# Two-layer hybrid trunk on one core: row sums of the layer norms and of the RMS norm moved by steps in the order of work

## The chip, the cores and the metric

The kernel runs on one core of a Trainium2 chip. The metric is the device time of one launch in microseconds (us), taken as the median of several runs. Before the change three runs gave 1219.54, 1220.56 and 1221.93 us. The engines are named as in the profile: PE is TensorE (PEld its weight loads), DVE is VectorE, ACT is ScalarE, POOL is GpSimd and SP issues the transfers.

## What is computed

The input x is 256 tokens by 1024 channels, in float32. Two layers follow each other, and a last RMS norm. Cut to what matters here, a layer is:

```
h = rms_norm(x, norm_w);  z = h @ w_in + b_in          # 20480 columns
y_ret  = (head_norm(retention(rq, rk, rv)) * ret_norm_w * silu(rg)) @ ret_w_o
y_att  = (merged_attention(aq, ak, av) * silu(ag)) @ att_w_o
c      = conv31(c_lin * sigmoid(c_gate)) + conv_dw_b
c      = silu(layer_norm(c, conv_norm_w, conv_norm_b))
y_conv = (c * silu(cg)) @ conv_w_o
gates  = sigmoid(mg)                                    # three times 1024 columns
x      = x + (gates0*y_ret + gates1*y_att + gates2*y_conv) @ w_out
```

Two norms matter for the change. `layer_norm` on the convolution's output c needs the mean of c over the 1024 channels of each token, then the mean of the squares of c less that mean. `rms_norm` at the start of layer 1 needs the mean of the squares of x, which exists only when layer 0 has ended.

## The kernel before

**Units.** All weights are cut into units of 256 columns by 1024 rows. `order()` writes the list of the units out by hand, per layer: cs0 cl0 cs1 cl1 cs2 cl2 (gate and linear half of the convolution's input), the units rq, rk, rv, rg, mr, yr of the retention, cs3 cl3, the units aq, ak, av, ma, ag of the attention, and at the end ya0 to ya3, mc0 to mc3, cg0 to cg3, yc0 to yc3 and wo0 to wo3. Here ya, yc and wo are the projections out of the attention, of the convolution and of the merged branches, mc is the merge gate of the convolution and cg its SiLU gate. The main loop goes through the list; unit n is the pair of a layer's kind and a number, and "step n" below is the loop's pass for unit n.

**A float32 product as three.** A weight tile is loaded (`raw`, issued by SP three steps ahead). `split(n + 2)` (L221, L222), two steps ahead, writes its rounded high part `whi` on ACT and the remainder `wlo` on DVE; there are five buffers of each half unit, so a cast waits until PE has left a buffer. The product then takes three matmuls for each tile: high by high, high by low and low by high. cs, cl, cg, rq and the like take 48 matmuls of 256 columns (L241, `gemm`); mr, ma, mc, yr, ya and yc go in couples of units and take 24 matmuls of 512 columns each (L275, `gemm_wide`), the first 12 for the first 128 tokens (t = 0) and the second 12 for the others (t = 1); wo goes in couples too (L298, `gemm_two`).

**What sets the order.** Each engine works its instructions off in the order in which the program writes them. Besides its own unit, a step carries out what was booked for it with `later(step, function, ..., at=queue)`. The queues are played at these places of a step: `after_split` right after the split of unit n + 2, `inside` in the middle of the unit's matmuls, `first` right behind its matmuls, `due` after the unit's results were taken out of PSUM, and `tail` at the end. In layer 1's step cs0 the split comes behind `first` (the flag `late`). `held` keeps the results of a unit in PSUM until `finish_held` takes them out. The convolution's 31 taps (L433) are put on DVE wherever a running credit allows it.

**Layer norm of c.** `ln_add` (L441 to L443) adds the channels on DVE, `ln_mean` lets PE sum over the partitions (`ss`, L326), scales the sum on DVE (`mean`, L448) and makes two diagonal matrices of it (`dg`, L347), and `ln_rows` lets PE spread them to all partitions (`rb`, L353). `ln_apply` (L457) then adds the row to c; `ln_square` squares on ACT (L361) and adds up on DVE (L363); `ln_rstd` does the sum, the power on POOL (L341) and the diagonals again, `ln_rows` the spreading, and `ln_apply` multiplies. In the last units cg0 to cg3, `gated` uses the result (L657).

**Change of layer.** `project` adds the product to x (`xt`, L701) after wo. Its inner function `rest` squares the new x (L361 on ACT, L363 on DVE) and splits x, times the norm's weight, into high and low part: `gx`, L373 on ACT and L374 on DVE. The first units of a layer work on this unscaled `gx`, so that they need not wait for the norm. `norm_diag` (`ss` on PE, `v` at L339, POOL, `dg`) and `norm_rows` (`rb` on PE, `rows` at L382 on ACT) make the norm's factor; `by_rstd` (`zr`, L403) applies it to the first units' results, and `scaled` (`hf` L392, `h` L395 and L313) writes the scaled input `h` for the units from rq0 on.

Of the kernel before, what the change touches and what calls it, by code (L numbers as in the profile page):

```python
# [13 lines left out]
ALU = mybir.AluOpType  # L14
# [28 lines left out]
C_ALL = C_MASK + 768  # L43

RATE = 3.0
H0 = ((2, (0, 2)), (4, (4, 6)))
H1 = ((1, (0, 2)), (3, (4, 6)))
UNSCALED = 3
WARM = 4

# [95 lines left out]
def trunk(ctx: ExitStack, tc, xp, wp, b_in, params, consts, out):  # L146
# [23 lines left out]
    pos = {u: n for n, u in enumerate(units)}  # L170
# [3 lines left out]
    first, inside, due, tail, after_split = (defaultdict(list) for _ in range(5))  # L174
    taps = []

    def later(n, fn, *a, at=due):
        at[n].append((fn, a))
# [137 lines left out]
    def pair_tile(name):  # L316
        return sb.tile([128, 2, S], F32, tag="tmp", name=name)
# [12 lines left out]
    def fold(v):  # L330
        DVE.tensor_tensor(v[:, 0], v[:, 0], v[:, 1], ALU.add)
        return v[:, 0]
# [23 lines left out]
    def add_squares(key, v, start, stop):  # L356

        if start:
            st[key] = sb.tile([128, 2, S], F32, tag="z", name="acc")
        sq = st[key] if start else pair_tile("sq")  # L360
        ACT.activation(sq, v, AF.Square)  # L361
        if not start:
            DVE.tensor_tensor(st[key], st[key], sq, ALU.add)  # L363
        if stop:
            st[key] = fold(st[key])

    def unscaled(l, k):

        if k == 0:
            st[l, "g"] = sb.tile([128, NK, 2, S], F32R, tag="gated", name="gx", bufs=1)  # L370
        g = st[l, "g"]
        w = col(l, P_NW + k) if l else xt[:, k:k + 1]
        ACT.mul(g[:, k, 0, :], x[:, k, :], w)  # L373
        DVE.scalar_tensor_tensor(g[:, k, 1, :], x[:, k, :], w, g[:, k, 0, :].bitcast(F32), ALU.mult, ALU.subtract)  # L374
# [323 lines left out]
    def project(l, i, n, p):  # L698
        k = 2 * i
        xs = x[:, k:k + 2]  # L700
        DVE.tensor_tensor(xs, p, xs, ALU.add)  # L701

        def rest():
            add_squares((l + 1, "sq"), xs, i == 0, i == 3)
            for q in range(2):
                unscaled(l + 1, k + q)
        if i < 2:
            later(n + 1, rest, at=after_split)
        else:
            rest()  # L710


    def turn_out(k):
# [83 lines left out]
    for l in range(DEPTH):  # L797
        for i in (0, 1, 2, 3):
            b = pos[l, "rq", i - i % 2]
            later(b + 3 + 2 * (i % 2), ret_scores, l, i)  # L800
            later(b + 6 + 2 * (i % 2), ret_out, l, i, at=first)
            later(b + 8 + 2 * (i % 2), ret_back, l, i, at=first)
        for pair in range(4):
            b = pos[l, "aq", pair]
            v = pos[l, "av", pair]
            for g in range(3):
                later(b + 2 * g + 3, att_scores, l, pair, g)
            later(v + 1, att_exp, l, pair)
            later(v + 2, att_share, l, pair)
            later(v + 4, att_turn, l, pair, 0, 0, at=first)  # L810
            later(v + 4, att_turn, l, pair, 0, 1, at=first)
            later(v + 5, att_pv, l, pair, 0, at=first)
            later(v + 5, att_turn, l, pair, 1, 0, at=first)
            later(v + 5, att_turn, l, pair, 1, 1, at=first)
            later(v + 6, att_pv, l, pair, 1, at=first)
        for part in range(2):
            later(pos[l, "yr", 3], by_residue, l, part, 0)
            later(pos[l, "cs", 3], by_residue, l, part, 4)
        y, c = pos[l, "ya", 0], pos[l, "mc", 0]
        later(y + 1, ln_add, l)  # L820
        later(y + 3, ln_mean, l, at=inside)
        later(y + 3, ln_rows, l)
        later(y + 3, ln_apply, l, ALU.add, (0, 2))
        later(y + 3, ln_square, l, (0, 2))
        later(c + 0, ln_apply, l, ALU.add, (4, 6))
        later(c + 0, ln_square, l, (4, 6))
        later(c + 1, ln_rstd, l)
        later(c + 2, ln_rows, l)
        later(c + 2, ln_apply, l, ALU.mult, (0, 2))
        later(c + 3, ln_apply, l, ALU.mult, (4, 6))  # L830
        b = pos[l, "cs", 0]
        if l:
            later(b, norm_diag, l, at=first)
            later(b + 1, norm_rows, l, at=first)
            later(b + 1, finish_held, at=first)
            for d, ks in H1:
                later(b + d, scaled, l, ks)
        else:
            later(b + 1, norm_diag, l, at=first)
            later(b + 2, norm_rows, l, at=inside)  # L840
            later(b + 2, finish_held, at=inside)
            for d, ks in H0:
                later(b + d, scaled, l, ks)

    def warm_up():

        z = sb.tile([128, S], F32, tag="bb", name="zero")
        DVE.memset(z, 0.0)
        p = ps.tile([128, S], F32, tag="S", name="warm", bufs=4)
        for _ in range(WARM):  # L850
            PE.matmul(p, z[:, 0:128], z, start=True, stop=True)
# [5 lines left out]
    with tc.manual_schedule():  # L857
        DVE.memset(mhalf, -0.5)
        warm_up()
        parts = ((0, 1), (1, 2), (2, 4), (4, 6), (6, 8))  # L860
        pieces = load(0, parts)
        for a, b in parts:
            lo, hi = (8 + a * S if a else 0), 8 + b * S
            SP.dma_start(xt[:, lo:hi], xp[:, lo:hi])
            next(pieces)
        all_of(pieces)
        all_of(load(1, ((0, 4), (4, 8))))
        SP.dma_start(cst[:, :C_COSR], consts[:, :C_COSR])
        SP.dma_start(prm[:, 0:P_CW], params[:, 0:P_CW])
        all_of(load(2))  # L870

        def prepare(a, b):
            for k in range(a, b):
                unscaled(0, k)
        split(0, parts, prepare)
        split(1)
        for k in (0, 2, 4, 6):
            add_squares((0, "sq"), x[:, k:k + 2], k == 0, k == 6)
        sg = sb.tile([128, 2], F32, tag="sm2", name="sg", bufs=4)
        ACT.activation(sg, mhalf, AF.Sigmoid)  # L880
        st["credit"] = 0.0
        for n, (l, kind, i) in enumerate(units):
            all_of(load(n + 3))
            if n == 0:
                SP.dma_start(prm[:, P_CW:], params[:, P_CW:])
                SP.dma_start(cst[:, C_COSR:C_DEC], consts[:, C_COSR:C_DEC])
            if n == 2:
                SP.dma_start(cst[:, C_DEC:], consts[:, C_DEC:])
            if kind == "av" and i < 4:
                bias_rows(l, units[n], AV + i * W)  # L890
            elif kind == "av" and i < 8:
                bias_rows(l, units[n], AV + i * W, AV + (i + 4) * W)
            elif kind in ("rv", "mr", "ma", "mc") and i % 2 == 0:
                bias_rows(l, units[n], COLS[kind][1] + i * W, COLS[kind][1] + (i + 1) * W)
            late = n < 3 or (kind, i) == ("cs", 0)
            if not late:
                split(n + 2)
            play(after_split, n)
            if kind in ("yr", "ya", "yc"):
                src = st[l, "gated"]  # L900
            elif kind == "wo":
                src = st[l, "mh"]
            elif kind == "aq" or kind in ("ak", "av") and i >= 4:
                src = st[l, "hp"]
            else:
                src = st[l, "g" if kind in ("cs", "cl") and i < UNSCALED else "h"]
            if n in couple:
                p = (gemm_two if kind == "wo" else gemm_wide)(n, src, lambda t, p: finish_half(n, t, p))
            elif kind == "av":
                p = gemm_values(n, src)  # L910
            else:
                p = gemm(n, src)
            play(first, n)
            if late:
                split(n + 2)
            if n < 2 or (kind, i) == ("cs", 0):
                held.append((n, p))
                continue
            if n not in couple:
                finish(n, p)  # L920
            elif couple[n][1]:
                finish_half(n, 1, p)
            play(due, n)
            st["credit"] = min(st["credit"] + RATE - COST[kind] - (0.6 if kind in ("cs", "cl") and i < UNSCALED else 0.0), 3.2)
            while taps and st["credit"] >= 0.79:
                fn, t = taps.pop(0)
                fn(t)
                st["credit"] -= 0.79
            play(tail, n)
        assert not (due or first or inside or taps), (list(due), len(taps))  # L930
# [44 lines left out]
```

## Time and profile before

| | |
|---|---|
| median of three runs | 1220.56 us |
| the profiled execution's own time | 1217.52 us |
| its span, first to last instruction | 1215.5 us |
| PE busy | 1197.6 us (99%), 8260 matmuls |
| DVE busy | 976.2 us (80%) |
| ACT busy | 751.1 us (62%) |
| transfers | 214.60 MB, 177 GB/s on the mean |
| mean granted clock of PE | 0.995 |

The profile is of one execution. A row of the timeline gives start, duration, engine, line, operation and `out<-in`, and in brackets the idle time ahead of it with what ended it. Consecutive alike instructions of an engine are merged into one row with a count. Matmuls are pipelined: one of 512 columns is listed with 0.39 us, though the next starts 0.23 us after it. So what a wait costs PE is read from start to start, less the usual distance. The granted clock has two levels here, 1.00 (2.4 GHz) and 0.50 (1.2 GHz).

### The profile page before, as it was taken

The numbers are of one execution on the slowest core, as the hardware profiler recorded it, in microseconds if no ns is written. First come the engines' busy times: TensorE is split into PE (matmuls) and PEld (weight loads), VectorE is DVE, ScalarE is ACT, GpSimd is POOL, SyncE is SP. The second block draws the span as 40 slices with busy tenths as digits, with TensorE's granted clock in tenths as the row PEclk, the third lists the DMA queues.
The fourth block names the chain that finished last, engine by engine and source line by source line (L and its number), as shares of the span: only waits on it lengthen the run. The fifth ranks groups of instructions, "written<-read, shape, count | busy, mean of one in ns | idle before, by whom it ended". The sixth has DMA issues, their size and how long they took to land.

```text
span 1215.5 us, 21472 instructions
## 1 busy us (share of the span) xinstructions
PE 1197.6 (99%) x8260; PEld 1116.8 (92%) x8260; DVE 976.2 (80%) x1702; ACT 751.1 (62%) x1116; POOL 9.2 (1%) x17
## 2 busy tenths in 40 slices
PE   9999999999999999999999999999999999999997
PEld 8999989999999989788999989899999999987987
DVE  6978799887888886766689787998887878767765
ACT  6635467878686756456455446586767686763652
POOL 0000000000000000000000000000000000000000
PEclk9999999999999999999999999999999999999999
DMA  8754576555555566555536564655555545565560
GB/s 301 239 191 134 162 210 195 164 182 162 165 177 167 160 191 182 182 180 179 187 123 190 165 196 138 213 191 169 174 162 175 163 168 168 185 182 182 184 189 35
DMA packets 129910, 214.60 MB, mean 177 GB/s; under 512 B 9872, under 2 KB 99728, under 8 KB 129680
## 3 DMA queue, kind: packets, MB, share of 16 engines
q1 hardware_dynamic: 129808, 213.24, 55.7%
q8 instruction: 64, 1.05, 0.3%
q14 instruction: 38, 0.31, 0.1%
HBM read 212.15 MB, written 1.05 MB: 175 GB/s over the span
## 4 chain that ended last, share of the span: by engine, by line
PE 90%; issue 7%; DVE 1%; ACT 1%; DMA 1%; SPq 0%; POOLq 0%; POOL 0%; DVEq 0%; ACTq 0%
PE g L241 47%; PE g L275 29%; PE g L256 4%; PE as L590 2%; PE g L298 2%; PE u L642 1%; PE pt L624 1%; PE rs L529 1%; PE u L637 1%; DVE wlo L222 0%; ACT whi L221 0%; DMA xt<-in_xp 0%; PE rs L531 0%; PE u L638 0%; PE rt L561 0%
## 5 line engine op out<-in xcount | busy, mean ns | idle before, releaser
L222 DVE TENSOR_TENSOR wlo<-raw,whi 128x1024 fp32r<-128x1024 f32 (+1 forms) x387 | 455.9, 1211 | 107.7 <-ACT whi L221 103.9
L221 ACT CAST whi<-raw 128x1024 fp32r<-128x1024 f32 (+1 forms) x387 | 391.8, 1042 | 197.9 <-PE g L275 109.1
L241 PE MATMUL g<-h,whi 128*128 128x256 f32 x1664 | 300.8, 283 | 0.0
L241 PEld LDWEIGHTS g<-h,whi 128*128 128x128 f32 x1664 | 257.3, 189 | 0.8
L241 PE MATMUL g<-h,wlo 128*128 128x256 f32 x832 | 235.1, 283 | 0.0
L241 PE MATMUL g<-hp,whi 128*128 128x256 f32 x1280 | 233.9, 285 | 0.0
L433 DVE SCALAR_TENSOR_TENSOR cacc<-cpad,prm,cacc 128x256 f32<-128x256 f32 x480 | 201.2, 477 | 0.5 <-ACT cacc L430 0.4
L241 PEld LDWEIGHTS g<-hp,whi 128*128 128x128 f32 x1280 | 200.3, 192 | 0.9
L241 PE MATMUL g<-hp,wlo 128*128 128x256 f32 x640 | 181.1, 283 | 0.0
L275 PE MATMUL g<-whi,h 128*128 128x512 f32 x512 | 166.3, 399 | 0.0
L241 PEld LDWEIGHTS g<-h,wlo 128*128 128x128 f32 x832 | 156.7, 188 | 0.0
L241 PEld LDWEIGHTS g<-hp,wlo 128*128 128x128 f32 x640 | 122.7, 192 | 0.0
L275 PE MATMUL g<-whi,gated 128*128 128x512 f32 x384 | 121.0, 391 | 0.0
L275 PEld LDWEIGHTS g<-whi,h 128*128 128x128 f32 x512 | 97.1, 190 | 21.9
L275 PE MATMUL g<-wlo,h 128*128 128x512 f32 x256 | 101.4, 396 | 0.0
L275 PEld LDWEIGHTS g<-whi,gated 128*128 128x128 f32 x384 | 72.1, 188 | 14.9
L275 PE MATMUL g<-whi,hp 128*128 128x512 f32 x256 | 82.3, 393 | 0.0
L241 PE MATMUL g<-gx,whi 128*128 128x256 f32 x384 | 73.0, 291 | 4.4 <-ACT gx L373 1.5
L500 DVE TENSOR_TENSOR zz<-zz,cst 128x512 f32<-128x512 f32 x48 | 33.2, 692 | 52.1 <-ACT zz L499 52.1
L275 PE MATMUL g<-wlo,gated 128*128 128x512 f32 x192 | 74.8, 389 | 0.0
L241 PEld LDWEIGHTS g<-gx,whi 128*128 128x128 f32 x384 | 61.6, 197 | 6.3 <-ACT gx L373 2.1
L497 ACT ACTIVATE z<-g,prm 128x256 f32<-128x256 f32 x96 | 45.6, 475 | 31.1 <-DVE cacc L433 12.0
(156 smaller groups left out, 1522.7 us busy)
## 6 DMA issues: line engine op xcount, KB each, us to landing
raw<-in_wp SPq DMA_DIRECT2D x222, 512.0 KB, 4.7
raw<-in_wp SPq DMA_DIRECT2D x323, 256.0 KB, 4.2
bb<-in_b_in SPq DMA_DIRECT2D x56, 128.0 KB, 4.3
cst<-in_consts SPq DMA_DIRECT2D x1, 1408.0 KB, 9.2
out_y<-o SPq DMA_DIRECT2D x4, 256.0 KB, 2.4
xt<-in_xp SPq DMA_DIRECT2D x3, 256.0 KB, 5.2
cst<-in_consts SPq DMA_DIRECT2D x1, 384.0 KB, 7.3
prm<-in_params SPq DMA_DIRECT2D x1, 360.0 KB, 6.9
```

What stands on the lines that cost most here:

```text
L221: ACT.copy(h, t)
L222: DVE.tensor_tensor(lo, t, h.bitcast(F32), ALU.subtract)
L241: PE.matmul(p[:, j], w, v, start=(k == 0 and i == 0 and j == 0), stop=(k == NK - 1 and i == 2 and j == 1))
L256: PE.matmul(p[:, j], a[:, k, u, r], v, start=(k == 0 and i == 0 and j == 0), stop=(k == NK - 1 and i == 2 and j == 1))
L275: PE.matmul(p, a[:, k, u, r], v, start=(k == 0 and i == 0), stop=(k == NK - 1 and i == 2))
L298: PE.matmul(parts[u][j], w, v, start=(k == 0 and i == 0 and (j == 0 or last)), stop=(k == NK - 1 and i == 2 and (j == 1 or last)))
L433: DVE.scalar_tensor_tensor(c[:, 2 * i + j], cp[:, j, t:t + S], col(l, P_TAP + (2 * i + j) * TAPS + t), c[:, 2 * i + j], ALU.mult, ALU.add)
L497: ACT.activation(z[:, j], p[:, j], AF.Identity, bias=b)
L500: DVE.tensor_tensor(zz, zz, two(cst[:, sin:sin + S]), ALU.mult)
L529: PE.matmul(s[:, 0:256], k[:, d, 0:128], q[:, d, :], start=(d == 0), stop=(d == 1))
L590: PE.matmul(s[:, r], q[:, j, t], k[:, j, t] if g else k[:, j, :], start=True, stop=True)
L624: PE.transpose(p[:, i, r * 128:r * 128 + 128], sm[:, r, o:o + 128], ident)
```

## The change

The layer norm's second and later parts are booked at other steps. With y the step of ya0 and c the step of mc0 (c = y + 4): the mean's row product goes from the end of step y + 3 into the middle of step c, the two additions of the row and the squares from y + 3 and c to the ends of the matmuls of c and c + 1, the variance from the end of step c + 1 to the middle of c + 3, its row product from the end of c + 2 to the middle of c + 4 (cg0), and the multiplications from c + 2 and c + 3 to step c + 4. This holds for both layers. At the change of layer, `rest` only splits x; the four squares of x are booked behind the matmuls of cs0 of the next layer. In layer 1 the norm's sum goes from behind cs0 into the middle of cl0, its row product from behind cl0 into the middle of cs1, cl0 is held like cs0, and the scaled `h` comes one step later (after steps cs1 and cs2). Layer 0's start stays as it was. No computation is added or left out.

```
-H0 = ((2, (0, 2)), (4, (4, 6)))
-H1 = ((1, (0, 2)), (3, (4, 6)))
+H = ((2, (0, 2)), (4, (4, 6)))
...
         def rest():
-            add_squares((l + 1, "sq"), xs, i == 0, i == 3)
             for q in range(2):
                 unscaled(l + 1, k + q)
         if i < 2:
             later(n + 1, rest, at=after_split)
         else:
             rest()
+        later(pos[l + 1, "cs", 0], add_squares, (l + 1, "sq"), xs, i == 0, i == 3, at=first)
...
         later(y + 3, ln_mean, l, at=inside)
-        later(y + 3, ln_rows, l)
-        later(y + 3, ln_apply, l, ALU.add, (0, 2))
-        later(y + 3, ln_square, l, (0, 2))
-        later(c + 0, ln_apply, l, ALU.add, (4, 6))
-        later(c + 0, ln_square, l, (4, 6))
-        later(c + 1, ln_rstd, l)
-        later(c + 2, ln_rows, l)
-        later(c + 2, ln_apply, l, ALU.mult, (0, 2))
-        later(c + 3, ln_apply, l, ALU.mult, (4, 6))
+        later(c + 0, ln_rows, l, at=inside)
+        later(c + 0, ln_apply, l, ALU.add, (0, 2), at=first)
+        later(c + 0, ln_square, l, (0, 2), at=first)
+        later(c + 1, ln_apply, l, ALU.add, (4, 6), at=first)
+        later(c + 1, ln_square, l, (4, 6), at=first)
+        later(c + 3, ln_rstd, l, at=inside)
+        later(c + 4, ln_rows, l, at=inside)
+        later(c + 4, ln_apply, l, ALU.mult, (0, 2), at=first)
+        later(c + 4, ln_apply, l, ALU.mult, (4, 6))
         b = pos[l, "cs", 0]
-        if l:
-            later(b, norm_diag, l, at=first)
-            later(b + 1, norm_rows, l, at=first)
-            later(b + 1, finish_held, at=first)
-            for d, ks in H1:
-                later(b + d, scaled, l, ks)
-        else:
-            later(b + 1, norm_diag, l, at=first)
-            later(b + 2, norm_rows, l, at=inside)
-            later(b + 2, finish_held, at=inside)
-            for d, ks in H0:
-                later(b + d, scaled, l, ks)
+        later(b + 1, norm_diag, l, at=inside if l else first)
+        later(b + 2, norm_rows, l, at=inside)
+        later(b + 2, finish_held, at=inside)
+        for d, ks in H:
+            later(b + d, scaled, l, ks)
...
-            if n < 2 or (kind, i) == ("cs", 0):
+            if kind in ("cs", "cl") and i == 0:
                 held.append((n, p))
                 continue
```

What this does to the order of the instructions is shown at three places. The changed file is one line shorter ahead of all of them, so each line number is one less there.

PE, layer 0, where ya3 ends and mc0 begins (`gated` is the input of ya, `h` that of mc), before:

```order
L275 MATMUL g<-wlo,gated 128x512
L275 MATMUL g<-whi,gated 128x512
L353 MATMUL rb<-dg,cst 128x128 x2
L275 MATMUL g<-whi,h 128x512
L275 MATMUL g<-wlo,h 128x512
```

PE, the same place after the change, in the middle of mc0:

```order
L274 MATMUL g<-whi,h 128x512 x2
L274 MATMUL g<-wlo,h 128x512
L274 MATMUL g<-whi,h 128x512
L352 MATMUL rb<-dg,cst 128x128 x2
L274 MATMUL g<-whi,h 128x512
```

The row product `rb` stood between ya3 and mc0; now the 12 matmuls of mc0's first half stand ahead of it.

DVE, layer 0, from the split of mc3 (before) to the last multiplication by the variance's row (`mg` is a merge gate, `gs` the SiLU gate of cg), before:

```order
L222 TENSOR_TENSOR wlo<-raw,whi 128x1024 x2
L669 TENSOR_TENSOR mg<-g,bb 128x512 x2
L339 TENSOR_SCALAR v<-ss 128x2
L347 TENSOR_SCALAR dg<-cst,r 128x128 x2
L222 TENSOR_TENSOR wlo<-raw,whi 128x1024 x2
L457 TENSOR_TENSOR cacc<-cacc,rb 128x512 x2
L222 TENSOR_TENSOR wlo<-raw,whi 128x1024 x2
L669 TENSOR_TENSOR mg<-g,bb 128x512 x2
L457 TENSOR_TENSOR cacc<-cacc,rb 128x512 x2
```

DVE, the same place after the change, from the splits of cg0 and cg1 on:

```order
L221 TENSOR_TENSOR wlo<-raw,whi 128x1024 x4
L668 TENSOR_TENSOR mg<-g,bb 128x512
L338 TENSOR_SCALAR v<-ss 128x2
L346 TENSOR_SCALAR dg<-cst,r 128x128 x2
L668 TENSOR_TENSOR mg<-g,bb 128x512
L221 TENSOR_TENSOR wlo<-raw,whi 128x1024 x2
L456 TENSOR_TENSOR cacc<-cacc,rb 128x512 x2
L656 TENSOR_TENSOR gs<-gs,cacc 128x512
L456 TENSOR_TENSOR cacc<-cacc,rb 128x512 x2
```

The variance's `v` and `dg` now stand behind the split of cg1, and the multiplications by its row stand among the work of cg0.

DVE at the change of layer, from the split of cl0 to the norm's sum, before:

```order
L222 TENSOR_TENSOR wlo<-raw,whi 128x1024 x2
L374 SCALAR_TENSOR_TENSOR gx<-xt,prm,gx 128x256 x2
L363 TENSOR_TENSOR acc<-acc,sq 128x512
L374 SCALAR_TENSOR_TENSOR gx<-xt,prm,gx 128x256 x2
L701 TENSOR_TENSOR xt<-g,xt 128x512
L363 TENSOR_TENSOR acc<-acc,sq 128x512
L374 SCALAR_TENSOR_TENSOR gx<-xt,prm,gx 128x256 x2
L701 TENSOR_TENSOR xt<-g,xt 128x512
L363 TENSOR_TENSOR acc<-acc,sq 128x512
L331 TENSOR_TENSOR acc<-acc 128x256
L374 SCALAR_TENSOR_TENSOR gx<-xt,prm,gx 128x256 x2
L339 TENSOR_SCALAR v<-ss 128x2
```

DVE, the same place after the change:

```order
L221 TENSOR_TENSOR wlo<-raw,whi 128x1024 x2
L373 SCALAR_TENSOR_TENSOR gx<-xt,prm,gx 128x256 x4
L700 TENSOR_TENSOR xt<-g,xt 128x512
L373 SCALAR_TENSOR_TENSOR gx<-xt,prm,gx 128x256 x2
L700 TENSOR_TENSOR xt<-g,xt 128x512
L373 SCALAR_TENSOR_TENSOR gx<-xt,prm,gx 128x256 x2
L362 TENSOR_TENSOR acc<-acc,sq 128x512 x3
L330 TENSOR_TENSOR acc<-acc 128x256
L221 TENSOR_TENSOR wlo<-raw,whi 128x1024 x4
L338 TENSOR_SCALAR v<-ss 128x2
L346 TENSOR_SCALAR dg<-cst,r 128x128 x2
```

The sums of squares moved behind the last `gx`, and four `wlo` (the splits of cs1 and cl1) moved ahead of `v`. ACT changes in the same way: eight `gx` in a row, then the four squares, then the casts.

## Rows read from the trace of the kernel before

**Rows 1.** What PE waited for: us in total, times, longest us.

```profile
PE rb L353 <- DVE dg L347: 5.7, 2, 2.8
PE g L241 <- ACT gx L373: 1.5, 3, 0.5
PE g L241 <- DVE gx L374: 1.5, 3, 0.8
```

**Rows 2.** Timeline of PE, layer 0, end of ya3 to mc0.

```profile
508.07 0.39 PE L275 MATMUL g<-whi,gated 128*128 128x512 f32 x1
...
511.29 1.19 PE L353 MATMUL rb<-dg,cst 128*128 128x128 f32 x4 [2.83 <-DVE dg L347]
...
514.95 0.39 PE L275 MATMUL g<-wlo,h 128*128 128x512 f32 x1
```

**Rows 3.** Timeline of DVE, layer 0, the same place.

```profile
510.67 0.15 DVE L448 TENSOR_SCALAR mean<-ss 128x2 f32<-128x2 f32 x1
510.85 0.48 DVE L347 TENSOR_SCALAR dg<-cst,mean 128x128 f32<-128x128 f32 x2
```

**Rows 4.** Timeline of PE, layer 1, the same place.

```profile
1112.81 0.68 PE L353 MATMUL rb<-dg,cst 128*128 128x128 f32 x4 [2.83 <-DVE dg L347]
...
1114.95 0.39 PE L275 MATMUL g<-wlo,h 128*128 128x512 f32 x1
...
1119.83 0.39 PE L275 MATMUL g<-wlo,h 128*128 128x512 f32 x1
```

**Rows 5.** Stretches behind both: length, busy of each engine, PEclk, DMA.

```profile
512.00:514.00 2.00, 2.00 (x8) 1.61 (x7) 1.86 (x3) 0.70 (x2) 0.00 (x0) 0.50 0.70 271
...
1112.00:1114.00 2.00, 1.20 (x7) 1.12 (x8) 1.93 (x6) 0.00 (x0) 0.00 (x0) 1.00 1.05 328
```

**Rows 6.** Timeline of PE, change of layer: end of wo3, cs0, cl0.

```profile
605.92 0.28 PE L298 MATMUL g<-mh,wlo 128*128 128x256 f32 x1
...
607.47 0.39 PE L241 MATMUL g<-gx,whi 128*128 128x256 f32 x1 [0.35 <-DVE gx L374]
...
614.95 0.39 PE L241 MATMUL g<-gx,whi 128*128 128x256 f32 x1 [0.80 <-DVE gx L374]
...
616.35 0.50 PE L326 MATMUL ss<-cst,acc 128*128 128x1 f32 x4
...
622.55 0.60 PE L353 MATMUL rb<-dg,cst 128*128 128x128 f32 x4
```

**Rows 7.** Timeline of ACT, change of layer.

```profile
604.70 1.05 ACT L221 CAST whi<-raw 128x1024 fp32r<-128x1024 f32 x1 [3.23 <-PE g L298]
...
606.19 0.89 ACT L373 ACTIVATE gx<-xt,prm 128x256 fp32r<-128x256 f32 x2
...
609.83 0.63 ACT L361 ACTIVATE sq<-xt 128x512 f32<-128x512 f32 x1 [1.42 <-DVE xt L701]
```

**Rows 8.** Timeline of DVE, change of layer and first units of layer 1.

```profile
606.93 0.88 DVE L374 SCALAR_TENSOR_TENSOR gx<-xt,prm,gx 128x256 fp32r<-128x256 f32 x2
607.72 0.69 DVE L363 TENSOR_TENSOR acc<-acc,sq 128x512 f32<-128x512 f32 x1
...
609.11 0.69 DVE L701 TENSOR_TENSOR xt<-g,xt 128x512 f32<-128x512 f32 x1
...
616.89 0.16 DVE L339 TENSOR_SCALAR v<-ss 128x2 f32<-128x2 f32 x1 [1.60 <-PE ss L326]
617.85 0.48 DVE L347 TENSOR_SCALAR dg<-cst,r 128x128 f32<-128x128 f32 x2 [0.80 <-POOL r L341]
618.25 4.62 DVE L222 TENSOR_TENSOR wlo<-raw,whi 128x1024 fp32r<-128x1024 f32 x4
...
639.43 1.67 DVE L392 SCALAR_TENSOR_TENSOR hf<-xt,prm,rows 128x256 f32<-128x256 f32 x4
641.01 1.46 DVE L313 TENSOR_TENSOR h<-hf,h 128x512 fp32r<-128x512 f32 x2
```

## The prediction

> **What bounds the kernel now.** I read the list of PE's waits first. PE is busy for 99% of the span, so time is won only where PE waits or runs at half clock. The list names two places: the mean's row product of the layer norm waited twice, 5.7 us together, for the diagonals from DVE; and the matmuls on `gx` waited six times, 3.0 us together, three times for ACT and three times for DVE [rows 1]. The first stands once in each layer, the second at the change of layer, the very places that the change edits. The starts of the matmuls show what these waits really cost, since the listed idle time leaves out the pipeline's refilling.
>
> *Layer norm.* The last matmul of ya3 starts at 508.07, the next instruction, `rb`, at 511.29 [rows 2]: 3.22 us, of which 0.23 is the usual distance, so 2.99 us are lost. Layer 1 has the same listed wait of 2.83 us [rows 4], so 2.99 again. DVE comes late because mean and diagonals stand in its queue behind a split and a merge: `mean` runs at 510.67, the diagonals end at 511.33 [rows 3].
>
> *Clock.* Behind this wait the clock is at 0.50 in layer 0 and at 1.00 in layer 1 [rows 5], though the wait was alike. From `rb` to the same later matmul PE took 514.95 - 511.29 = 3.66 us in layer 0 and 1114.95 - 1112.81 = 2.14 us in layer 1 [rows 2, 4]. The half clock cost 1.52 us.
>
> *Change of layer.* cs0 could have begun at 605.92 + 0.12 = 606.04 and ended at 616.35 [rows 6]: 10.31 us. From there, `ss` with its 0.36 us of distance and cl0 took until 622.55, so a unit takes (6.20 - 0.36)/48 = 0.12 us per matmul or 5.75 us unhindered. cs0 lost 10.31 - 5.75 = 4.56 us. The pattern behind it: `gx` of channels 0 to 3 is behind the split of cl0 on both engines; for the next channels, squares and their additions stand between the addition to x and `gx` [rows 7, 8].
>
> **The change part by part.**
>
> *1. The mean's row in the middle of mc0.* A 512-column matmul takes (1119.83 - 1114.95)/21 = 0.232 us [rows 4]. mc0 can start at 508.30, its first 12 matmuls end at 511.09. `rb` still starts when its diagonals allow it, at 511.29, since nothing ahead of them on DVE moved. Left of the wait: 0.20 us. The work of `rb` is the same before and after.
>
> *2. The variance's row in the middle of cg0.* It cost PE no wait before. Now `v` stands behind the split of cg1 and a merge gate. The second cast of cg1 needs a buffer that mc3 leaves at three quarters of its matmuls. From there: cast 1.05 [rows 7], `wlo` 4.62/4 = 1.16, merge gate 0.69 as for an addition of the same size, and from `v` to the end of `dg` 618.33 - 616.89 = 1.44 [rows 8], with hand-overs of about 0.1: 4.4 us. PE needs for its way to `rb` six matmuls of mc3 and half of cg0: 1.39 + 2.87 = 4.26 us. Left: a wait of 0.15 us. Below, it is 0 if the buffer is free earlier; above, about 1.2 if one more `wlo` comes in late. I take 0.17, nearest to the sum.
>
> *3. Applications and squares one or two steps later.* They lie on DVE and ACT beside PE's work. What needs them is yc0, four cg units of 5.75 us after the row product; the DVE work between is two multiplications and four products with `cg`, all below 1 us each. I cost it at nothing; its cover is these 20 us, and a delay would show as a wait of yc1 for `gated`. The two layer norms together give 2 x (2.99 - 0.20 - 0.17) = 5.2 us, and the half clock of layer 0 goes with its wait: 1.5 us.
>
> *4. Squares out of the way of gx.* The cast of cl0 ends at 605.75 [rows 7]; `gx` of channel 0 now begins there instead of at 606.19. That brings nothing: its low part starts on DVE at 606.93, behind a `wlo`, as before, and PE goes on at 607.47 as before [rows 6, 8]. By then 607.47 - 606.04 - 0.12 = 1.31 us are lost. From 607.47 on: four low parts end at 608.6; the third addition to x, which began at 609.11 behind an addition of squares, ends at 609.2; ACT, now without a square of 0.63 in front, has the next `gx` at 609.7 (0.47 each), DVE the low part at 610.2. PE gets to channel 4 at about 610.3: no wait, where two stood. The fourth addition ends at 611.2, `gx` at 611.7, its low part at 612.2; PE is at channel 6 at 611.75 and can go on with the low part at 612.28, by the same 0.53 from DVE's start to PE as in 606.93 to 607.47. It loses 0.4 us. The rest of cs0 takes 616.35 - 614.95 = 1.40 as before [rows 6], so cs0 ends at 613.68 instead of 616.35: **2.7 us**.
>
> *5. The norm's sum and row one half unit later in order.* ACT squares from 612.1 on (four at 0.62), DVE adds behind `gx`, three of 0.69 and a fold: done at about 615.8. PE reaches `ss` in the middle of cl0 at 613.68 + 2.87 = 616.55: no wait. Then four `wlo` (4.62 us) go ahead of `v`: to 620.4; with 1.44 the diagonals are there at 621.8. PE reaches `rb` in the middle of cs1 at 613.68 + 5.75 + 0.36 + 2.87 = 622.7: no wait, 0.9 us to spare.
>
> *6. Scaled h a step later, cl0 held.* No instruction is added. rq0 needs h of channels 4 to 7 at its middle: PE is there at about 646.0 (622.7 + 0.4 for `rb`, half of cs1, four units until rq0, which is entered at 643.1, and half of rq0). On DVE, from 622 on: the split of cs2, two `zr`, `cpad`, a `zr`, `hf` 1.67, `h` 1.46 [rows 8], three taps, two splits, and the rest of cl1 and cs2, gives `hf` at 641 to 643.7 and the last low part at 645.1; before it was at 642.5. The order is a step later, PE 2.7 us earlier; 1.5 us are left for channel 4. I cost it at nothing. SP's queue keeps its order; the raw tile of cs2's second half waits for the `wlo` of cs1, which now comes at about 616.9 instead of 619.4, so it is not later.
>
> Sum: 5.2 + 1.5 + 2.7 = 9.4 us. Against the profiled execution, 1217.52, this is 1208.1. The median of the runs shown is 3.04 us above that execution; nothing in the change's places explains that, so I carry it: **1211.1 us**.
>
> **A rule against a row.** Two waits of 2.83 us, one followed by half clock and one not [rows 4, 5]: what a wait costs in clock is not a property of the program alone. The Trainium skill, page "TensorE: Matmul & The Clock Gate", section "What's actually happening", says that the gate's counting runs free of the kernel's start, so that the point at which the clock changes varies. The trace agrees as far as two waits can.
>
> **The rivals.**
>
> *A. The clock did otherwise in the timed runs.* If none of them has a half-clock stretch, the gain is 7.9 us (1212.7); if both layers have one, 10.9 (1209.6). The rows show each case once, so for two waits one stretch is the likeliest; runs spread by 2.4 us.
>
> *B. The gain at the change of layer is given back.* DVE has little spare time from cs0 to rk1; if `hf` or a split comes more than 1.5 us later than in part 6, rq0 waits, and 2.7 us go at most: 1213.8. For it: `v` behind four `wlo`, `scaled` a step later. Against it: the sums above.
>
> *C. The rows' waits only move.* If `rb` in mc0 or in cg0 found its diagonals as late as today relative to PE, only the change of layer and perhaps the clock would be won: 1217.9 to 1216.3. Against it: DVE's queue ahead of the first diagonals is unchanged and PE has 2.8 us more work before them.
>
> *D. The change doesn't do what it says.* The squares need only x, so in ACT's queue they start right behind `gx`, not after cs0. Should they wait for cs0's end, `ss` comes 0.8 to 1.6 us late: 1212 to 1213.
>
> *E. Slower: DVE becomes the bound at layer 1's start.* A lack there is paid at rq0's middle, in one piece. To lose 9.4 us and 2.4 more, DVE must be 1.5 + 11.8 = 13.3 us later than in part 6, two and a half units' worth. Nothing in the rows comes near: the last low part of `h` moves by 2.6 us.
>
> **How the numbers follow.** A change below 0.2% (2.4 us) can't be told from none in a measurement of this kernel. Forecast with all parts 0.60; A 0.14; B 0.12; C 0.05; D 0.03; E 0.04; 0.02 for small waits that eat the sum. The range reaches from A with its larger gain, less 2 us for the bounds of parts 1, 2 and 4, to between B and C: 1207.5 to 1216.5. Faster: forecast, A, B, D and a part of C: 0.90; same: the rest of C and the last: 0.06; slower: E: 0.04.
>
> **What would show it.** The waits of `rb` for `dg` fall from 5.7 us to below 1, in mc0 and cg0; no half clock before the kernel's end; the waits for `gx` go from 3.0 us to below 2, with none left at channel 4; cs0 takes 7.6 us; squares start before cs0's end; no wait at rq0. Wrong would be: a new wait above 1 us at `rb` in cg0 or cs1, at rq0 or at yc1.

## The result and the profile after

The changed kernel takes 1207.99 us (median of four runs, 1207.48 to 1208.45) against 1220.14 us for the kernel before (1219.54 to 1221.93) beside it: a ratio of 0.9905, 95% interval 0.9890 to 0.9919, so 12.15 us or 1.0% less. The forecast was 1211.1 us, 9.4 us less. The profiled execution after took 1207.90 us with a span of 1206.0 us. Against the profiled execution before, the span fell by 9.5 us, where the prediction's sum has 9.4; the timed runs fell by 2.7 us more. The 1207.99 us lie in the predicted range, 0.5 us above its lower end.

The list of PE's waits after the change (us in total, times, longest us):

```profile
PE g L240 <- ACT whi L220: 1.9, 2, 1.6
PE warm L843 <- DVE zero L840: 1.2, 1, 1.2
PE g L240 <- DVE gx L373: 0.9, 1, 0.9
PE g L240 <- DVE wlo L221: 0.8, 2, 0.6
```

Against [rows 1], the waits of `rb` for `dg` are gone from the list. Of six listed waits for `gx` one is left. The other rows belong to the first units of the launch.

The timeline of PE in layer 0, at the two row products of the layer norm:

```profile
510.79 0.40 PE L274 MATMUL g<-whi,h 128*128 128x512 f32 x1
511.21 0.68 PE L352 MATMUL rb<-dg,cst 128*128 128x128 f32 x4
...
534.48 0.28 PE L240 MATMUL g<-h,wlo 128*128 128x256 f32 x1
534.91 0.68 PE L352 MATMUL rb<-dg,cst 128*128 128x128 f32 x4
```

Both stand without listed idle time. From start to start the first loses 0.42 - 0.23 = 0.19 us, the second 0.43 - 0.12 = 0.31 us (0.19 and 0.30 in layer 1). DVE's rows for the two pairs of diagonals:

```profile
510.78 0.48 DVE L346 TENSOR_SCALAR dg<-cst,mean 128x128 f32<-128x128 f32 x2
...
533.43 0.15 DVE L338 TENSOR_SCALAR v<-ss 128x2 f32<-128x2 f32 x1
534.47 0.48 DVE L346 TENSOR_SCALAR dg<-cst,r 128x128 f32<-128x128 f32 x2 [0.90 <-POOL r L340]
```

The mean's diagonals come 0.07 us earlier than in [rows 3]: nothing about them became faster, PE only has 12 matmuls to do in the meantime. PE could have gone on with the second row at 534.60; the pair of the variance's diagonals is made from 534.47 to 534.95, and `rb` starts at 534.91.

The change of layer, PE, to be held against [rows 6]:

```profile
601.71 0.28 PE L297 MATMUL g<-mh,wlo 128*128 128x256 f32 x1
602.00 0.38 PE L240 MATMUL g<-gx,whi 128*128 128x256 f32 x1
603.25 0.39 PE L240 MATMUL g<-gx,whi 128*128 128x256 f32 x1 [0.87 <-DVE gx L373]
...
612.46 0.50 PE L325 MATMUL ss<-cst,acc 128*128 128x1 f32 x4
...
618.66 0.60 PE L352 MATMUL rb<-dg,cst 128*128 128x128 f32 x4
```

`ss` now stands in the middle of cl0, so cs0 ended 24 matmuls, 2.87 us, earlier: at 609.59. It began at 601.83 and took 7.76 us, against 10.31 before. And the queues that feed it, ACT and then DVE, against [rows 7] and [rows 8]:

```profile
601.45 1.70 ACT L372 ACTIVATE gx<-xt,prm 128x256 fp32r<-128x256 f32 x4
605.02 0.92 ACT L372 ACTIVATE gx<-xt,prm 128x256 fp32r<-128x256 f32 x2 [1.88 <-DVE xt L700]
607.09 0.91 ACT L372 ACTIVATE gx<-xt,prm 128x256 fp32r<-128x256 f32 x2 [1.15 <-DVE xt L700]
607.90 0.62 ACT L360 ACTIVATE acc<-xt 128x512 f32<-128x512 f32 x1
```

```profile
602.72 1.67 DVE L373 SCALAR_TENSOR_TENSOR gx<-xt,prm,gx 128x256 fp32r<-128x256 f32 x4
604.30 0.69 DVE L700 TENSOR_TENSOR xt<-g,xt 128x512 f32<-128x512 f32 x1
605.56 0.89 DVE L373 SCALAR_TENSOR_TENSOR gx<-xt,prm,gx 128x256 fp32r<-128x256 f32 x2 [0.58 <-ACT gx L372]
...
616.28 0.15 DVE L338 TENSOR_SCALAR v<-ss 128x2 f32<-128x2 f32 x1
617.24 0.48 DVE L346 TENSOR_SCALAR dg<-cst,r 128x128 f32<-128x128 f32 x2 [0.81 <-POOL r L340]
...
638.68 1.46 DVE L312 TENSOR_TENSOR h<-hf,h 128x512 fp32r<-128x512 f32 x2
```

The squares start at 607.90, while cs0 still runs; nothing makes them wait for it. The norm's diagonals end at 617.72, 0.9 us ahead of the `rb` that needs them. The scaled input is complete at 640.14, ahead of rq0's middle at about 642.2.

### The profile page after: what moved, and what is told of

It reads as the page before. It is cut to its first block, busy times and chain, and to the rows that moved or that the text cites. A ratio compares the mean times of both kernels' runs of the same rounds, so it can differ in the third digit from the quotient of the medians.

```text
span 1206.0 us, 21474 instructions
## 1 busy us (share of the span) xinstructions
PE 1194.5 (99%) x8260; PEld 1113.6 (92%) x8260; DVE 975.7 (81%) x1702; ACT 750.9 (62%) x1116; POOL 9.2 (1%) x17
## 4 chain that ended last, share of the span: by engine, by line
PE 91%; issue 6%; DVE 1%; DMA 1%; ACT 1%; SPq 0%; POOLq 0%; POOL 0%; DVEq 0%
PE g L240 47%; PE g L274 31%; PE g L255 4%; PE as L589 2%; PE g L297 2%; PE u L641 1%; PE pt L623 1%; DMA raw<-in_wp 1%; PE rs L528 1%; PE u L636 1%; ACT whi L220 0%; PE rs L530 0%; PE u L637 0%; PE rt L560 0%; PE r L540 0%
```

## Experiments

Two questions were left: where the 2.7 us come from that the timed runs won beyond the profile, and which moves the gain hangs on. Each kernel ran beside the kernel before on one chip: e1, e2, e3 and e5 share a median before of 1219.35 us (28 runs), the other four one of 1219.14 us (17 runs).

**The kernel before against itself (e1).** No edit.

> The kernel before, unchanged, against itself. Open: its timed runs (median 1220.14 us) lie 2.6 us above its profiled execution (1217.52), while those of the changed kernel lie at its own (1207.99 against 1207.90). Theory 1 (half clock): the timed runs hold more half-clock stretches behind PE's waits than the one, of 1.52 us, in the profiled execution; then runs differ by steps of about 1.5 us and the longer a run, the lower its mean granted clock (each such stretch takes about 0.0014 off 0.995 or more). Theory 2 (something outside the waits, such as transfers at the start): runs are longer at an unchanged mean clock.

It took 1218.34 us, ratio 0.9994 (0.9983 to 1.0004). Sorted by mean granted clock, the 40 runs of it (12 and the 28 beside) have these spans:

```
mean granted clock   runs   span, us
0.997 to 0.998          4   1214.1 to 1215.1
0.994 to 0.996         25   1215.0 to 1217.9
0.992 to 0.993         11   1218.2 to 1219.1
```

Sorted like this, the lower the clock, the longer the runs, as theory 1 has it; the steps of 1.5 us that it also foresaw are blurred. One trace against another need not follow this order: the trace of before has 1215.5 us at 0.995, that of this run 1216.8 us at 0.996. The mean also counts half clock at the start of the launch, which the first has (first row) and the second has not:

```profile
10.00:12.00 2.00, 2.00 (x11) 2.00 (x11) 1.80 (x5) 1.68 (x4) 0.00 (x0) 0.50 1.02 402
10.00:12.00 2.00, 2.00 (x17) 2.00 (x18) 2.00 (x5) 1.89 (x5) 0.00 (x0) 1.00 1.05 422
```

Both come to the first `ss` of the launch at 20.58 us all the same. Over the ten traces this moment lies between 20.2 and 21.1 us; so up to 0.9 us of the spread lies there, outside the waits, as theory 2 has it.

The profiled run of this kernel shows one more thing: the same wait of 2.83 us in layer 1, at 1.00 behind it in [rows 5], now has this behind it (stretches as there, then PE's timeline):

```profile
1112.00:1114.00 2.00, 2.00 (x7) 1.71 (x7) 1.94 (x4) 0.59 (x1) 0.00 (x0) 0.50 0.96 297
1114.00:1116.00 2.00, 2.00 (x6) 1.52 (x6) 1.09 (x2) 1.57 (x3) 0.00 (x0) 0.50 0.11 45
1116.00:1118.00 2.00, 2.00 (x8) 1.54 (x7) 0.83 (x1) 0.00 (x0) 0.00 (x0) 0.63 0.08 18
```

```profile
1111.40 1.19 PE L353 MATMUL rb<-dg,cst 128*128 128x128 f32 x4 [2.83 <-DVE dg L347]
...
1121.21 0.39 PE L275 MATMUL g<-wlo,h 128*128 128x512 f32 x1
```

This is the same matmul as the one at 1119.83 in [rows 4]: 9.81 us from `rb` here, 7.02 there. The half clock cost 2.79 us, where it cost 1.52 in layer 0 of the trace of before. One wait of one length is followed by a stretch that costs nothing, 1.5 or 2.8 us.

**Filling the wait instead of moving the work (e5).**

```
+    def fill(l):
+        p = ps.tile([128, 512], F32, tag="S", name="fill", bufs=4)
+        g = st[l, "gated"]
+        for _ in range(12):
+            PE.matmul(p, g[:, 0, 0, 0:128], g[:, 0, :, :], start=True, stop=True)
...
+        later(y + 3, fill, l)
         later(y + 3, ln_rows, l)
```

> The kernel before with 12 matmuls of 512 columns, whose result nobody reads, put on PE ahead of the mean's row product in both layers, where PE waits 2.99 us. They take 12 x 0.232 = 2.8 us, so PE loses the same time but is not idle. Theory 1: no half clock behind them; timed 1220.1 - 1.5 - 2.6 = 1216.0, span 1214.0 or less. Theory 2: only the one stretch of the profiled execution can go: 1218.6. If the clock is none of it: 1220.1, or a little more for the added matmuls.

Measured: 1216.09 us, ratio 0.9978 (0.9968 to 0.9988), 3.26 us below the kernel before. The time is that of theory 1; but the kernel before beside it was faster than the 1220.1 us from which both theories start, and as a saving 3.26 us stands between the 4.1 of theory 1 and the 1.5 of theory 2, with an interval from 1.5 to 3.9. The spread and the clock in the trace speak for theory 1, and so do the traces set side by side further below. Its span is 1213.9 us. Its ten runs lie within 1.8 us, those of the kernel before beside them within 5.1. PE in layer 0, then a stretch behind the filler in each layer:

```profile
508.20 2.88 PE L456 MATMUL fill<-gated 128*128 128x512 f32 x12
511.19 0.68 PE L354 MATMUL rb<-dg,cst 128*128 128x128 f32 x4
```

```profile
512.00:514.00 2.00, 2.00 (x10) 1.64 (x9) 1.76 (x3) 0.80 (x2) 0.00 (x0) 1.00 0.73 243
1112.00:1114.00 2.00, 2.00 (x10) 1.65 (x9) 1.78 (x3) 0.79 (x2) 0.00 (x0) 1.00 0.87 302
```

`rb` starts 6.2 us behind the `ss` ahead of it, as before, and no useful work moved; 24 matmuls that compute nothing are worth 3.3 us because PE is not idle. So in the timed runs the half clock behind the two layer norms costs a median run some 3.3 us (1.5 to 3.9 by the interval), where the profiled execution held 1.5.

**The layer norm's steps alone (e2).** The change's block of ten `later` lines, with the rest of the kernel before.

> Only the layer norm's steps are moved, the change of layer is as before. By the prediction's sum in rows 5.2 us of waits and 1.5 us of half clock go: span 1208.8. In timed runs, by theory 1 with the extra half clock behind the two layer norms: 1220.1 - 6.7 - 2.6 = 1210.8; if the extra half clock lies at the change of layer, or by theory 2: 1213.4. Rival (the layer norm's gain is not the larger part): above 1216.

1211.09 us, ratio 0.9932 (0.9918 to 0.9947): 8.26 us less. The time is at the first of the two values expected; the saving lies between the 9.3 and the 6.7 us that they stand for, and its interval (6.5 to 10.0) holds both, so this run doesn't decide between the theories. That the layer norm's part is the larger one is shown. In its waits `rb` is gone and `gx` is as before:

```profile
PE g L241 <- ACT gx L373: 1.5, 3, 0.5
PE g L241 <- DVE gx L374: 1.5, 3, 0.8
```

**The change of layer alone (e3).** The rest of the change, with the layer norm as before.

> Only the change of layer is moved, the layer norm's steps are as before. By the sum 2.7 us in the rows of cs0, and the two waits of 2.83 us at the layer norms stay. Timed: 1217.4 if the extra half clock lies at the layer norms or outside; 1214.8 if it lies at the change of layer.

1215.78 us, ratio 0.9974 (0.9963 to 0.9984): 3.57 us less, between the two values. The interval (2.0 to 4.5 us) holds the 2.7 us of the first and not the 5.3 of the second. Its runs spread over 4.9 us, as those of the kernel before do, and both waits of `rb` are still listed, 5.7 us. PE's timeline has the last matmul of wo3 and the `ss` in the middle of cl0, and the clock falls behind both layer norms (stretches as above):

```profile
606.23 0.28 PE L297 MATMUL g<-mh,wlo 128*128 128x256 f32 x1
...
616.98 0.50 PE L325 MATMUL ss<-cst,acc 128*128 128x1 f32 x4
```

```profile
512.00:514.00 2.00, 2.00 (x7) 1.73 (x8) 1.97 (x4) 0.25 (x1) 0.00 (x0) 0.50 1.00 369
1112.00:1114.00 2.00, 2.00 (x6) 1.57 (x5) 1.30 (x3) 1.44 (x3) 0.00 (x0) 0.50 0.45 154
```

cs0 takes 616.98 - 2.87 - 606.35 = 7.76 us, as in the changed kernel. Around the change of layer the clock is 1.00 in this trace and in that of before, so the extra half clock is not there. The two halves together give 8.26 + 3.57 = 11.8 us, the whole change 12.15 and 10.9 in its two measurements.

**The changed kernel again (e8).** No edit.

> The changed kernel, unchanged, on the chip of the runs beside it. 1207.99 us as in its first runs, all within 1 us of each other, since no wait of PE is left at the layer norms behind which the clock could fall.

1208.21 us, ratio 0.9913 (0.9901 to 0.9926), within 0.9 us of each other. The gain is 10.9 us on this chip.

**The mean's row alone (e6).** The variance and the multiplications go back to the steps they had, and so do the second of the two additions and its squares.

```
         later(c + 0, ln_rows, l, at=inside)
         later(c + 0, ln_apply, l, ALU.add, (0, 2), at=first)
         later(c + 0, ln_square, l, (0, 2), at=first)
-        later(c + 1, ln_apply, l, ALU.add, (4, 6), at=first)
-        later(c + 1, ln_square, l, (4, 6), at=first)
-        later(c + 3, ln_rstd, l, at=inside)
-        later(c + 4, ln_rows, l, at=inside)
-        later(c + 4, ln_apply, l, ALU.mult, (0, 2), at=first)
-        later(c + 4, ln_apply, l, ALU.mult, (4, 6))
+        later(c + 0, ln_apply, l, ALU.add, (4, 6))
+        later(c + 0, ln_square, l, (4, 6))
+        later(c + 1, ln_rstd, l)
+        later(c + 2, ln_rows, l)
+        later(c + 2, ln_apply, l, ALU.mult, (0, 2))
+        later(c + 3, ln_apply, l, ALU.mult, (4, 6))
```

> The changed kernel with only the first row product of the layer norm moved (into the middle of mc0, with the two additions it feeds); the variance and the multiplications keep the steps that they had before. If the gain at the layer norm is that one wait and its clock, as the prediction has it, this is as fast as the changed kernel: 1208.0, within 0.5. If the later steps of the variance and the multiplications are needed too (the rival: DVE comes too late for the row product behind mc2, or for cg0), a wait of 0.5 to 3 us stands there in each layer: 1209 to 1214.

1211.91 us, ratio 0.9946 (0.9932 to 0.9959): 3.7 us slower than the changed kernel. The rival holds, but at another place than it named. The first row is of PE's waits, the others of PE's timeline in layer 0:

```profile
PE ss L325 <- DVE acc L330: 2.6, 2, 1.3
```

```profile
520.35 0.40 PE L274 MATMUL g<-whi,h 128*128 128x512 f32 x1
522.07 0.58 PE L325 MATMUL ss<-cst,acc 128*128 128x1 f32 x4 [1.32 <-DVE acc L330]
```

It is not the row product but the sum over the partitions behind mc1. The squares are summed up 10.3 us behind `rb` here and 10.5 us in layer 1 of the kernel before; but PE, which did half of mc0 ahead of `rb` instead of standing still, now gets to `ss` 8.9 us behind `rb` instead of 11.7. From start to start 1.72 - 0.23 = 1.5 us go in each layer, 3.0 us in all; the second row product, back behind mc2, gives 0.6 of them back. The spans of the two traces differ by 3.4 us, of which 0.6 stand ahead of the first `ss` of the launch (20.97 against 20.42 us). The six runs spread over 3.0 us; whether the clock fell behind the new wait in some of them is not shown, for in the trace it didn't.

**gx ahead of the squares, in the same step (e7).**

```
         def rest():
-            add_squares((l + 1, "sq"), xs, i == 0, i == 3)
             for q in range(2):
                 unscaled(l + 1, k + q)
+            add_squares((l + 1, "sq"), xs, i == 0, i == 3)
```

> The kernel before, with only the two parts of the function after project exchanged: gx ahead of the squares, but both still in the steps of wo. If the order within a step were enough, cs0 would take 7.75 us in the rows, as in the changed kernel. By the queue sums the additions of squares still stand between the additions to x on DVE: gx of channel 4 comes 0.45 and that of channel 6 about 1.05 us earlier than before, and PE then waits about 0.2 us for the norm's sum: cs0 takes 9.2 us, against 10.3 before. Timed 0.9 us below the kernel before, if the clock behind the layer norms leaves that to be seen.

1218.10 us, ratio 0.9991 (0.9982 to 1.0000), 1.0 us less, which the interval hardly tells from none. The rows tell it. PE, then DVE:

```profile
606.33 0.28 PE L298 MATMUL g<-mh,wlo 128*128 128x256 f32 x1
...
613.59 0.91 PE L241 MATMUL g<-gx,whi 128*128 128x256 f32 x2 [0.69 <-ACT gx L373]
...
615.70 0.61 PE L326 MATMUL ss<-cst,acc 128*128 128x1 f32 x4
```

```profile
611.70 0.69 DVE L363 TENSOR_TENSOR acc<-acc,sq 128x512 f32<-128x512 f32 x1
612.31 0.68 DVE L701 TENSOR_TENSOR xt<-g,xt 128x512 f32<-128x512 f32 x1
```

From 606.45 to `ss` 9.25 us pass, as expected. An addition of squares still stands in front of the last addition to x on DVE, and `gx` of channel 6 waits for that. The exchange is worth 1.1 of the 2.6 us; the rest needs the squares behind every `gx`.

**The split of cl0 behind gx too (e4).** On top of the changed kernel:

```
             late = n < 3 or (kind, i) == ("cs", 0)
-            if not late:
+            last = (kind, i) == ("wo", 3)
+            if not late and not last:
                 split(n + 2)
...
+            if last:
+                split(n + 2)
             play(due, n)
```

> A version that may beat both: the changed kernel, with the split of cl0 put behind the last gx of wo's last step instead of ahead of the first. The 1.4 us that cs0 still loses at its first channels, where gx stands behind that split on both engines, and the 0.4 us at channel 6 should go: cs0 takes 5.8 us in the rows, 1206.2 timed. Rival: the later split of cl0 delays its remainder on DVE beyond the end of cs0, or the squares and the norm's row behind it; then a wait for cl0's split or for the diagonals takes the place, and it stays at 1207 to 1209.

1206.39 us, ratio 0.9899 (0.9884 to 0.9913). Its five runs, 1206.25 to 1206.54, lie all below those of the changed kernel on the same chip, 1207.79 to 1208.66: 1.8 us less, as expected, and the fastest of all kernels here. ACT's `gx`, PE's last matmul of wo3, the first of cs0 and `ss` in cl0:

```profile
598.22 1.71 ACT L372 ACTIVATE gx<-xt,prm 128x256 fp32r<-128x256 f32 x4 [1.89 <-DVE xt L700]
```

```profile
602.19 0.28 PE L297 MATMUL g<-mh,wlo 128*128 128x256 f32 x1
602.31 0.40 PE L240 MATMUL g<-gx,whi 128*128 128x256 f32 x2
...
610.94 0.50 PE L325 MATMUL ss<-cst,acc 128*128 128x1 f32 x4
```

cs0 follows wo3 at the usual 0.12 us and takes 610.94 - 2.87 - 602.31 = 5.76 us. No wait for `gx` is listed any more. In the changed kernel the first `gx` stood on ACT behind this cast, which waited for a weight buffer that wo had to leave:

```profile
600.49 1.05 ACT L220 CAST whi<-raw 128x1024 fp32r<-128x1024 f32 x1 [3.23 <-PE g L297]
```

It stood behind the cast, not behind anything that it needs.

## Why the prediction was right, and where it was short

**The bounds.** The two places were the right ones, and the waits were worth what the starts of the matmuls said. Predicted 9.4 us against the profiled execution, 9.5 measured in the spans.

**Part 1** (0.20 us left at the first row product): 0.19. **Part 2** (0.17 at the second): 0.31; the chain of cast, `wlo`, merge gate, `v` and diagonals was found as the bound that it is, 0.1 us longer.

**Part 3** said that the applications and squares cost nothing, with yc0 as the place where it would show. The cost was right, the reason incomplete. The mean's row alone, with the variance at its old step, lost 3.0 us in the rows at the variance's sum and 3.7 timed: with PE's stop gone, the squares became the next thing that came late. Moving the variance is what keeps the gain, not a move that happens to be free.

**Part 4** (2.7 us at cs0): 10.31 - 7.76 = 2.55 in the rows, in the trace of the change of layer alone as in that of the whole change. What it said of the first channels, that nothing is won there, holds: the wait of 0.87 us is the one left over, and the last experiment shows that the split ahead of it is the cause.

**Parts 5 and 6** (0.9 us and 1.5 us to spare): 0.9 and about 2; no wait at `ss`, at `rb` in cs1 or at rq0. Rivals B, C, D and E did not come about.

**What fell short** is the step "nothing in the change's places explains that, so I carry it", on the 3.04 us between the profiled execution and the median. For the larger part (3.3 - 1.5 = 1.8 us) it was half clock behind the layer norm's waits, the very thing priced at 1.52 us in the paragraph on the clock, and the change's places do explain it. One execution showed one stretch; the fill experiment puts a median run at 3.3 us. The four traces that still have the wait say much the same. From `rb` to the `ss` after mc1 PE takes, in us:

```
                              layer 0   layer 1
before                          13.19     11.67
before again (e1)               11.67     14.46
change of layer alone (e3)      13.03     13.23
gx ahead of the squares (e7)    13.24     13.27
waits filled (e5)               11.67     11.67
```

11.67 us is the stretch at full clock. Of eight waits of one length six were followed by half clock, five times at a cost of 1.4 to 1.6 us and once of 2.8; that is 2.6 us in an execution on the mean. Take what each trace has of it, and its time to the first `ss` of the launch, from its span, and 1193.4, 1193.5 and 1193.4 us remain of before, e1 and e5, and 1185.6 and 1185.8 of the changed kernel's two traces: 7.5 to 7.9 us less, where the rows give 2 x (2.99 - 0.19 - 0.31) + 2.55 = 7.5. In these traces nothing larger than 0.4 us is left to explain.

With 3.3 in the place of 1.5 the sum is 5.2 + 3.3 + 2.7 = 11.2 us, against 12.15 measured at first (9.9 to 13.4 by the interval) and 10.9 when the changed kernel ran again. Rival A was the right mechanism with too small a price: it counted stretches of one length, at most one to a layer, and took one of two waits for the likeliest. The page named there, "TensorE: Matmul & The Clock Gate" of the Trainium skill, says in "What's actually happening" that the gate's counting doesn't start with the kernel, and that the point at which the clock changes varies. The eight waits agree in this: their lengths are the same, and what followed them is not.

Part of the 12.15 us is luck of the sample: the kernel before had 1220.14 us as the median of four runs, and 1219.35 and 1219.14 us as the medians of 28 and 17 runs later. Against these 1207.99 us would be 11.4 and 11.2 us less. Whether the chips differ too is not shown.

## What to carry to other kernels

When an engine that bounds the kernel waits, put work that is ready between the wait's producer and its consumer: half a unit of matmuls here hid 3 us without making anything faster. Then look for what comes late next, since the chain behind the wait was timed by it. Price a wait of TensorE over several runs and not from one trace: the half clock that followed a wait of 2.99 us here cost up to 2.79, and a difference between the profiled and the timed runs may be just that.

## What the runs showed of the hardware

A wait of 2.83 us on PE, the same in length each time and seen eight times in four traces, was followed by no half clock (twice), by one that cost 1.4 to 1.6 us (five times), or by one that cost 2.79 us (once). Filling the wait with matmuls that compute nothing made the kernel 3.26 us faster (1.5 to 3.9 by the interval), and its runs spread over 1.8 us where those of the kernel before spread over 5.1. The waits at the change of layer, 3.0 us in six pieces over 10 us, showed no half clock behind them in the four traces that hold them (before, e1, e2, e5). In seven of the ten traces PE ran at half clock for a time between 8 and 14 us of the launch; these came to the first `ss` after 20.5 to 21.1 us, the other three after 20.2 to 20.6.
